# Seven products of block sums in layer 0's last product as well, and later TensorE steps for mLSTM's sums

## The chip, the cores and the metric

The kernel runs on one core of a Trainium2 chip, as one launch. The metric is the device time of that launch in microseconds (us). TensorE (PE in the profile) multiplies; VectorE (DVE), ScalarE (ACT) and GpSimd (POOL) do the elementwise work; SyncE (SP) issues nearly all DMAs, in the order in which they were put into its queue. Every engine works through its instructions in order.

## The reference

The program is a decoder trunk of two residual layers on 256 tokens of width 1024, in float32. Layer 0 mixes the tokens with an mLSTM of 4 heads, layer 1 with causal attention of 8 heads; a SwiGLU network with 2816 hidden columns stands behind each.

```python
for layer in range(2):
    u = rmsnorm(h, norm_mix[layer])
    y = mlstm_mixer(u, ...) if layer == 0 else moba_mixer(u, ...)
    h = h + y
    h = h + swiglu(rmsnorm(h, norm_ffn[layer]), ffn_w_in[layer], ffn_w_out[layer])

def swiglu(u, w_in, w_out):
    gt, up = jnp.split(u @ w_in, 2, axis=-1)
    return (jax.nn.silu(gt) * up) @ w_out
```

In the mLSTM, sums over time of the forget gates and a running maximum give the decay weights of each head; those weigh the products of queries and keys, which then multiply the values. "Layer 0's last product" is `(silu(gt) * up) @ w_out` of layer 0: 256 rows by 2816 by 1024.

## The kernel before

**Numbers.** Every factor of a large product is held as two float16 parts, a high one and a low one, and each block product is three matmuls of 512 columns: high times high, high times low, low times high. Weights come from memory as float32 pieces of 128x2048 (tile `raw`, 5 buffers). ScalarE writes a piece's high part (`wh`), VectorE its low part (`wl`), 1024 columns at a time; both have 8 buffers. `Weights.ahead` runs while the program is being written out and puts these loads and conversions between the other work. A counter `owed` says how many pieces may be loaded, each time a buffer has been read for good. `take` hands out the next converted pieces and `free` gives their buffers back.

**The order of the work.** The program is written in the order in which TensorE works. `Pace` keeps an estimated clock of TensorE (`pace.now`) and of the other engines. A `Chain` is a row of steps on several engines; each is put into its engine's queue when by these estimates its input is ready. `pace.when(test, fn)` runs `fn` as soon as the test holds at the estimated time. `follows` uses it for the mLSTM's small steps that need TensorE: `cumsum` (tile `pf`), `cummax` (`pr`), four `decay` steps (`arg`), `maxcol` (`pm`), each after the chain of the step before. They are put between the matmuls of the key and value projections (`ak`, `av`); `scores` (`qk`) and `attend_a` (`num`, `den`) come behind them.

**The feed-forward network.** `ffn(l, ...)` computes 11 groups of 256 hidden columns for both halves of the tokens (`hidden`, tile `gu`: a float32 product `fh`, its parts `n` on ScalarE and VectorE, and one transposing DMA into `hT`). Then follows the last product over 11 pieces of 256 hidden columns (tiles `f0o` and `f1o`): pieces 0 to 6 for all four blocks of the output, 2 by 2 of 128 rows by 512 columns, and then four tail pieces, first for token half 0 and then for half 1, so that the residual sum and the next norm of half 0 run beside the tail of half 1. Layer 1's projections (`b`) come right behind.

**Seven products.** A plain piece is a product of 2 by 2 blocks by 2 by 2 blocks: eight block products, 24 matmuls. In layer 1, pieces 0, 1, 3 and 5 (`SEVEN`) take seven block products of sums of blocks instead (`block`, 21 matmuls, on the four output banks and on four more, `win...`). The sums of the weights' blocks are made by VectorE from the float32 piece into a `raw` buffer of their own (`Weights.add`, four subtractions) and converted as a piece of their own (a `None` in `specs`). The sums of the hidden blocks are made in `sums_of` (tile `fs`, four steps, then the parts and a transposing DMA into `hsT`). At the end a chain named `more` adds the four extra banks onto the residual.

Of the kernel before, what the change touches and what calls it, by code (L numbers as in the profile page):

```python
# [12 lines left out]
F16 = mybir.dt.float16  # L13
# [7 lines left out]
P = 128  # L21
# [31 lines left out]
RAWBUFS, WBUFS = 5, 8  # L53


SEVEN = (0, 1, 3, 5)


START = [
# [150 lines left out]
def trunk(ctx: ExitStack, tc: tile.TileContext, a: dict, out: bass.AP):  # L210
    pace = Pace()
# [45 lines left out]
    for w, cols in ((wa, (VCOL, 0, A_SQ, VCOL + 512, OCOL, OCOL + 512)), (wb, [g * SB + i * 512 for i, g in  # L257
                    ((0, 0), (0, 1), (1, 0), (1, 1), (0, 2), (1, 2))])):
        l = 0 if w is wa else 1
        specs += [in_rows(w, c, half) for c in cols for half in range(2)]  # L260
        specs += [out_rows((a["a_w_out"], a["b_w_out"])[l][0], i) for i in range(KD // 2)]
        specs += [ffn_rows(a["ffn_w_in"][l], f, half) for f in range(NFF // 2) for half in range(2)]
        for i in range(NFF // 2):
            specs.append(out_rows(a["ffn_w_out"][l], i))
            if l == 1 and i in SEVEN:

                summed.add(len(specs))
                specs.append(None)

    class Weights:  # L270
# [24 lines left out]
        def add(self):  # L295

            i, j = self.adds.pop(0)
            (b11, b12, b21, b22), t = ([r[:, x * 512:(x + 1) * 512] for x in range(4)] for r in self.raws[i - 1:i + 1])
            x, y = ((b12, b11), (b22, t[0]), (b22, b12), (b21, t[1]))[j]
            nc.vector.tensor_tensor(t[j], x, y, op=ALU.subtract)  # L300
            self.landed[i] = pace.end

        def half(self, n):

# [11 lines left out]
        def low(self):  # L316

            i, sl = self.lows // 2, self.half(self.lows)
            h, l = self.parts[i]
            nc.vector.scalar_tensor_tensor(l[:, sl], self.raws[i][:, sl], WS, h[:, sl], op0=ALU.mult, op1=ALU.subtract)  # L320
            self.lows += 1
            self.owed += 1 - self.lows % 2

        def load_owed(self, whole=False):
            if self.owed and len(self.raws) < len(specs):
# [392 lines left out]
    part = pa.tile([A_H, S], BF16, name="part")  # L718
    mtodo, mdone = [], {}

    def follows(name, made, chain=None, test=None):


        def run():
            mdone[name] = made()

        job = pace.when(lambda: (chain is None or chain() is not None and chain().through()) and (test is None or test()), run)
        mtodo.append((name, job, chain))

    def ensure(name):  # L730
# [193 lines left out]
    for g in range(2):  # L924
        w = ws.take_k(2, 4)
        for t in range(NT):
            b = xbank(f"a{'qk'[g]}{t}")
            proj_tok(b, u, w, t)
            qk_done(g, t, b)
            if (g, t) == (0, 0):  # L930
                nc.vector.tensor_scalar(gh, gr, WS, None, op0=ALU.mult)
                nc.vector.scalar_tensor_tensor(gl, gr, WS, gh, op0=ALU.mult, op1=ALU.subtract)
            if (g, t) == (0, 1):
                prev = "gates"
                mdone["gates"] = gates()
                for name, made in [("cumsum", cumsum), ("cummax", cummax)] + [
                        (f"arg{h}", lambda h=h: decay(h)) for h in range(A_H)] + [("maxcol", maxcol)]:
                    follows(name, made, lambda prev=prev: mdone.get(prev))
                    prev = name
        ws.free(2)  # L940

# [98 lines left out]
    def ffn(l, u, j1, u_next, gain, middle):  # L1040
# [8 lines left out]
        def hidden(f, t, w):  # L1049
            b = (xbank, ybank)[t](f"gu{l}{f}{t}")  # L1050
            proj_tok(b, u, w, t, steps=3)
            sg = pfp.tile([P, 256], F32, tag="fsg", bufs=2, name=f"fsg{l}{f}{t}")
            nc.scalar.activation(sg, b[:, 0:256], AF.Silu, scale=1.0 / PS)
            seven = l == 1 and f in SEVEN
            hf = pfp.tile([P, 256], F32, tag="fhs" if seven else "fh", bufs=4, name=f"fh{l}{f}{t}")
            hfs[f, t] = hf

            h2 = []

            def prod():  # L1060
                nc.vector.scalar_tensor_tensor(hf, b[:, 256:512], HS / PS, sg, op0=ALU.mult, op1=ALU.mult)

            def high():
                h2.append(new16()[:, 0:512])
                nc.scalar.activation(h2[0][:, 0:256], hf, AF.Copy)

            def low():
                nc.vector.tensor_tensor(h2[0][:, 256:512], hf, h2[0][:, 0:256], op=ALU.subtract)
                flip16(hT[:, f, :, t * P:(t + 1) * P], h2[0])

            hjobs[f, t] = Chain(pace, [("DVE", prod), ("ACT", high), ("DVE", low)])
            if seven and t == 1:
                hjobs[f, 1].then = lambda: sums_of(f)

        def sums_of(f):

            x = pfp.tile([P, 512], F32, tag="fs", bufs=2, name=f"fs{f}")
            n16 = new16()

            def add():  # L1080
                (a11, a12), (a21, a22) = ([hfs[f, t][:, j * P:(j + 1) * P] for j in range(2)] for t in range(NT))
                s = [x[:, j * P:(j + 1) * P] for j in range(4)]
                for d, y, z, op in ((s[0], a21, a22, ALU.add), (s[1], s[0], a11, ALU.subtract),
                                    (s[2], a11, a21, ALU.subtract), (s[3], a12, s[1], ALU.subtract)):
                    nc.vector.tensor_tensor(d, y, z, op=op)

            def low():
                nc.vector.tensor_tensor(n16[:, 512:1024], x, n16[:, 0:512], op=ALU.subtract)
                flip16(hsT[:, SEVEN.index(f)], n16)

            sjobs[f] = Chain(pace, [("DVE", add), ("ACT", lambda: nc.scalar.activation(n16[:, 0:512], x, AF.Copy)),
                                    ("DVE", low)])


        hjobs, hfs, sjobs = {}, {}, {}
        if l == 1:
            hsT = pfp.tile([P, len(SEVEN), 8, P], F16, name="hsT")
        w = []
        for t in range(NT):
            if t == 1:  # L1100
# [16 lines left out]
        banks = [[xbank(f"f{l}o{t}{n}") for n in range(2)] for t in range(NT)]  # L1117
        npc, tail = NFF // 2, 4
        scale = 1.0 / (WS * HS)
        seven = SEVEN if l == 1 else ()  # L1120
        plain = [i for i in range(npc - tail) if i not in seven]
        begun, more = set(), {}

        def block(key, y, w, last):

# [8 lines left out]
        for i in range(npc - tail):  # L1134
            if i in seven:
# [6 lines left out]
                    [(h[:, j * 512:(j + 1) * 512], lo[:, j * 512:(j + 1) * 512]) for j in range(4)] for h, lo in pieces)  # L1142
                a11, a12 = ([x[:, 0:P] for x in hid(2 * i + j)] for j in range(2))
                a22 = [x[:, P:S] for x in hid(2 * i + 1)]
                s1, s2, s3, s4 = ([hsT[:, SEVEN.index(i), 4 * x + j, :] for x in range(2)] for j in range(4))
                end = i == seven[-1]
                for key, y, w in (("p1", a11, b11), ((0, 0), a12, b21), ((0, 1), s4, b22), ((1, 0), a22, t4),
                                  ("p6", s2, t2), ("p7", s3, t3), ("p5", s1, t1)):
# [37 lines left out]
        for t in range(NT):  # L1186
            last_layer = u_next is None
            ss = None if last_layer else new_ss(t)
            sums = []
            for ns in ((0, 1),) if t == 0 else ((0,),) if last_layer else ((0,), (1,)):  # L1190
                for j in range(2 * tail):
                    k = k0 + j
                    if len(w) <= j:
                        w += ws.take_k(1, 2)
                    hjobs[k // 2, t].finish()
                    acc_chunk(banks[t], *hid(k), w[j], t, False, k == NFF - 1, ns)
                for n in ns:
                    sums.append(residual_half(t, n, banks[t][n], scale, ss))
                    if last_layer:
                        sl = slice(n * 512, (n + 1) * 512)  # L1200
                        nc.sync.dma_start(orow[t * P:(t + 1) * P, sl], hres[t][:, sl])
            if last_layer and t == 1:

                more.finish()
                residual_half(1, 1, banks[1][1], scale)
                bs = [ybank(f"end{q}") for q in range(2)]
                for j in range(2 * tail):
                    (yh, yl), (wh, wl) = hid(k0 + j), w[j]
                    for q in range(2):
                        sl = slice(512 + q * 256, 768 + q * 256)  # L1210
                        for i, (lhs, rhs) in enumerate(((yh, wh), (yh, wl), (yl, wh))):
                            mm(bs[q][:, 0:256], lhs[:, P:S], rhs[:, sl], j == 0 and i == 0, j == 2 * tail - 1 and i == 2)
                for q, queue in enumerate((nc.sync, nc.scalar)):
                    sl = slice(512 + q * 256, 768 + q * 256)
                    nc.vector.scalar_tensor_tensor(hres[1][:, sl], bs[q][:, 0:256], scale, hres[1][:, sl],
                                                   op0=ALU.mult, op1=ALU.add)
                    queue.dma_start(orow[P:S, sl], hres[1][:, sl])
            if not last_layer:
                if job is not None:
                    job()  # L1220
                job = norm(f"f{l}", t, ss, grow, u_next, sums)
# [267 lines left out]
```

## Time and profile before

| What | us |
|---|---|
| Median of 3 runs | 543.25 |
| Lowest and highest of them | 542.76 to 544.75 |
| The profiled execution's own time | 543.92 |
| Its span, first to last instruction | 542.2 |
| TensorE's share of the span, busy | 99% |

The profiled execution is one execution; its span leaves out 1.7 us ahead of the first and behind the last instruction. Matmul durations overlap in the profile: a matmul of 512 columns is shown with 379 ns, and the next one starts sooner than that, so starts are compared here and not durations.

### The profile page before, as it was taken

What the parts mean: (1) busy time and instruction counts of PE and PEld (TensorE: products, weight loads), DVE (VectorE), ACT (ScalarE), POOL (GpSimd) and SP (SyncE); (2) the same over time, 40 slices, a digit from 0 to 9 for tenths busy, and PEclk for the clock granted to TensorE, in tenths of its full rate; (3) what the DMA queues carried; (4) which work ended last, traced back from release to release, by engine and by line L of the source; (5) the groups of instructions that cost most, each with busy time, mean ns of one, the idle gap of its engine ahead of it and who ended that gap; (6) DMA issues with size and microseconds to landing.
All of it is one profiled execution on the core that took longest, in us unless ns stands there. A gap on an engine that the chain in (4) does not pass through costs nothing.

```text
span 542.2 us, 7899 instructions
## 1 busy us (share of the span) xinstructions
PE 534.5 (99%) x2678; PEld 253.3 (47%) x2678; DVE 386.3 (71%) x599; ACT 317.2 (59%) x556; POOL 46.0 (8%) x105
## 2 busy tenths in 40 slices
PE   8989999999999999999999999999999999999997
PEld 4445644444444444444444455544444444444444
DVE  5979679588766655673358778988875665889932
ACT  6787584476455555463268996847655364555600
POOL 4400220010300000000013311000000000000000
PEclk9999999999999999999999999999999999999999
DMA  8999749969699879999329969699689989898502
GB/s 295 365 297 303 267 125 249 317 178 243 151 270 236 243 222 230 249 378 384 136 49 228 269 147 243 166 310 241 163 201 255 191 222 248 251 224 266 177 0 79
DMA packets 143081, 122.88 MB, mean 227 GB/s; under 512 B 68616, under 2 KB 113936, under 8 KB 143040
## 3 DMA queue, kind: packets, MB, share of 16 engines
q1 hardware_dynamic: 142144, 119.97, 80.5%
q0 software_dynamic: 736, 2.27, 1.5%
q8 instruction: 21, 0.34, 0.3%
q14 instruction: 20, 0.16, 0.1%
q10 hardware_dynamic: 160, 0.14, 0.1%
HBM read 106.08 MB, written 1.05 MB: 198 GB/s over the span
## 4 chain that ended last, share of the span: by engine, by line
PE 86%; DMA 7%; DVE 3%; issue 2%; ACT 1%; SPq 0%; POOL 0%; POOLq 0%; DVEq 0%; ACTq 0%
PE gu L228 40%; PE f0o L228 11%; PE b L228 8%; PE f1o L228 7%; PE ao L228 6%; DMA raw<-in_a_w_in 6%; PE bv L228 4%; PE av L228 2%; PE winp L228 2%; PE bo L228 1%; DVE wl L184 1%; DMA u_f<-n 1%; PE end L228 1%; PE s L228 1%; PE ak L228 1%
## 5 line engine op out<-in xcount | busy, mean ns | idle before, releaser
L184 DVE SCALAR_TENSOR_TENSOR wl<-raw,wh 128x1024 f16<-128x1024 f32 (+1 forms) x208 | 243.2, 1196 | 36.9 <-ACT wh L184 36.2
L184 ACT ACTIVATE wh<-raw 128x1024 f16<-128x1024 f32 (+1 forms) x208 | 207.8, 1029 | 82.2 <-DMA raw<-in_ffn_w_in 38.3
L228 PE MATMUL gu<-wh,u_f 128*128 128x512 f16 x704 | 209.9, 379 | 0.6 <-DMA u_f<-n 0.6
L228 PEld LDWEIGHTS <-u_f 128*128 128x128 f16 x1056 | 103.2, 98 | 125.4 <-DMA u_f<-n 1.1
L228 PE MATMUL gu<-wl,u_f 128*128 128x512 f16 x352 | 133.4, 379 | 0.0
L228 PEld LDWEIGHTS <-h 128*128 128x128 f16 x492 | 48.1, 98 | 53.1
L228 PE MATMUL f0o<-wh,h 128*128 128x512 f16 x176 | 46.6, 379 | 0.0
L184 DVE SCALAR_TENSOR_TENSOR fh<-gu,fsg 128x256 f32<-128x256 f32 x44 | 18.6, 423 | 35.0 <-ACT fsg L184 34.9
L228 PEld LDWEIGHTS <-u_a 128*128 128x128 f16 x336 | 28.7, 98 | 31.2 <-issue 0.8
L228 PEld LDWEIGHTS <-u_b 128*128 128x128 f16 x288 | 27.8, 98 | 32.0
L228 PE MATMUL b<-wh,u_b 128*128 128x512 f16 x128 | 38.9, 379 | 0.0
L184 ACT ACTIVATE n<-fh 128x256 f16<-128x256 f32 x44 | 18.2, 414 | 28.4 <-DVE fh L184 23.1
L228 PE MATMUL f1o<-wh,h 128*128 128x512 f16 x112 | 31.8, 379 | 0.0
L228 PE MATMUL f0o<-wl,h 128*128 128x512 f16 x88 | 27.4, 379 | 0.0
L184 ACT ACTIVATE fsg<-gu 128x256 f32<-128x256 f32 x44 | 16.4, 373 | 18.3 <-PE gu L228 18.2
L184 DVE TENSOR_TENSOR n<-fh,n 128x256 f16<-128x256 f32 x44 | 18.6, 423 | 10.2 <-ACT n L184 10.1
L228 PE MATMUL b<-wl,u_b 128*128 128x512 f16 x64 | 24.3, 379 | 0.0
L184 ACT ACTIVATE junk<-x 128x512 f32<-128x512 f32 x14 | 8.8, 629 | 25.2 <-DVE x L184 23.3
L184 POOL TENSOR_TENSOR r<-s,mhalf 128x1 f32<-128x1 f32 x8 | 4.5, 562 | 215.1 <-DVE s L184 215.1
L228 PE MATMUL bv<-wh,u_b 128*128 128x512 f16 x64 | 20.0, 379 | 0.0
L228 PE MATMUL ao<-wh,u_a 128*128 128x512 f16 x64 | 19.8, 379 | 0.0
L228 PE MATMUL av<-wh,u_a 128*128 128x512 f16 x64 | 19.7, 379 | 0.0
(208 smaller groups left out, 539.0 us busy)
## 6 DMA issues: line engine op xcount, KB each, us to landing
raw<-in_ffn_w_in SPq DMA_DIRECT2D x176, 256.0 KB, 4.5
raw<-in_ffn_w_out SPq DMA_DIRECT2D x88, 256.0 KB, 4.4
raw<-in_a_w_in SPq DMA_DIRECT2D x48, 256.0 KB, 5.5
raw<-in_b_w_in SPq DMA_DIRECT2D x48, 256.0 KB, 5.4
raw<-in_a_w_out SPq DMA_DIRECT2D x16, 256.0 KB, 5.7
raw<-in_b_w_out SPq DMA_DIRECT2D x16, 256.0 KB, 4.0
x<-in_x SPq DMA_DIRECT2D x4, 256.0 KB, 3.3
grow<-in_norm_ffn POOLq DMA_DIRECT2D x2, 512.0 KB, 5.4
```

The costliest lines, as they stand in the source:

```text
L184: return fn(*args, **kw)
L228: nc.tensor.matmul(dst, lhsT, rhs, start=start, stop=stop)
```

## The change

`SEVEN` becomes a pair, one tuple for each layer, and layer 0 has the same four pieces as layer 1. So `specs` gets four more pieces of weight sums in layer 0, `hidden` keeps float32 products for `sums_of` there, `hsT` exists in both layers, and the loop of the last product takes the branch with seven products. `more.finish()` moves ahead of the residual sums. `owed` is counted differently: a piece whose blocks are summed counts as read only when its four subtractions are put out too. `follows` gets a `slack`: a step is put out not when its input is ready by the estimate, but 1.5 us (`cumsum`) or 0.4 us (the other six) later.

```diff
-SEVEN = (0, 1, 3, 5)
+SEVEN = ((0,1,3,5),(0,1,3,5))
...
-            if l == 1 and i in SEVEN:
+            if i in SEVEN[l]:
                 summed.add(len(specs))
                 specs.append(None)
...
             nc.vector.tensor_tensor(t[j], x, y, op=ALU.subtract)
             self.landed[i] = pace.end
+            if j == 3 and self.lows >= 2 * i:
+                self.owed += 1
+
+        def summing(self, i):
+            return i + 1 in summed and (i + 1 >= len(self.raws) or any(q[0] == i + 1 for q in self.adds))
...
             self.lows += 1
-            self.owed += 1 - self.lows % 2
+            if self.lows % 2 == 0 and not self.summing(i):
+                self.owed += 1
...
-    def follows(name, made, chain=None, test=None):
+    def follows(name, made, chain, slack):
...
-        job = pace.when(lambda: (chain is None or chain() is not None and chain().through()) and (test is None or test()), run)
+        job = pace.when(lambda: chain() is not None and chain().through() and pace.now >= chain().ready + slack, run)
...
-                    follows(name, made, lambda prev=prev: mdone.get(prev))
+                    follows(name, made, lambda prev=prev: mdone.get(prev), 1.5 if name == "cumsum" else 0.4)
...
-            seven = l == 1 and f in SEVEN
+            seven = f in SEVEN[l]
...
-        if l == 1:
-            hsT = pfp.tile([P, len(SEVEN), 8, P], F16, name="hsT")
+        if SEVEN[l]:
+            hsT = pfp.tile([P, len(SEVEN[l]), 8, P], F16, name="hsT")
...
-        seven = SEVEN if l == 1 else ()
+        seven = SEVEN[l]
...
                     acc_chunk(banks[t], *hid(k), w[j], t, False, k == NFF - 1, ns)
+                if more:
+                    more.finish()
                 for n in ns:
                     sums.append(residual_half(t, n, banks[t][n], scale, ss))
...
             if last_layer and t == 1:
-                more.finish()
                 residual_half(1, 1, banks[1][1], scale)
```

## Rows read from the trace of the kernel before

**Rows 1.** The page: the span, the busy time of the engines (share of the span, instructions), TensorE's granted clock in 40 equal slices (9 is 90% or more of full speed), and the shares of the chain that ended last.
```profile
span 542.2 us, 7899 instructions
PE 534.5 (99%) x2678; PEld 253.3 (47%) x2678; DVE 386.3 (71%) x599; ACT 317.2 (59%) x556; POOL 46.0 (8%) x105
...
PEclk9999999999999999999999999999999999999999
...
PE 86%; DMA 7%; DVE 3%; issue 2%; ACT 1%; SPq 0%; POOL 0%; POOLq 0%; DVEq 0%; ACTq 0%
```

**Rows 2.** The chain that ended last, in order of time: start, us, what. First layer 0's hidden products and its last product, then the start of layer 1's last product.
```profile
106.30 113.96 PE gu L228 x528
220.26 56.98 PE f0o L228 x264
...
484.16 0.65 PE winp L228 x3
```

**Rows 3.** Busy time of each engine (instructions in brackets) in four stretches: pieces 0 to 6 of layer 0's last product, from its first matmul to the first of the tail; its tail, to the first matmul of `b`; pieces 0 to 6 of layer 1's last product, from its first matmul to the first of the tail; layer 0's hidden products. Columns: stretch, length, then PE, PEld, DVE, ACT, POOL, TensorE's granted clock, DMA share, GB/s.
```profile
220.10:256.36 36.26, 36.26 (x170) 16.45 (x169) 21.32 (x19) 18.21 (x19) 0.00 (x0) 1.00 0.96 338
256.36:277.08 20.72, 20.72 (x98) 9.38 (x97) 7.23 (x10) 6.38 (x11) 0.57 (x1) 1.00 0.45 137
484.00:517.67 33.67, 33.67 (x157) 15.25 (x156) 33.16 (x40) 19.36 (x23) 0.00 (x0) 1.00 0.64 208
100.00:220.00 120.00, 119.83 (x558) 54.40 (x557) 81.04 (x116) 67.79 (x102) 8.42 (x34) 1.00 0.88 229
```

**Rows 4.** Groups of instructions by shape, with busy us, mean ns and idle time before them: TensorE's weight loads (PEld) in pieces 0 to 6 of layer 0 (the first row) and of layer 1 (the other two).
```profile
L228 PEld LDWEIGHTS <-h 128*128 128x128 f16 x167 | 16.4, 98 | 19.7
...
L228 PEld LDWEIGHTS <-h 128*128 128x128 f16 x107 | 10.5, 98 | 12.6
L228 PEld LDWEIGHTS <-hsT 128*128 128x128 f16 x48 | 4.7, 98 | 5.7
```

**Rows 5.** Groups by shape over the whole run: what the four pieces with seven products cost VectorE and ScalarE in layer 1 (two kinds of the weights' low parts, of 1024 and of 512 columns; one of the two groups of the weights' sums; one of the four groups of the hidden sums; their two parts; one group of the four extra banks' way onto the residual), and the issues of the transposing DMA with the median us to landing.
```profile
L184 DVE SCALAR_TENSOR_TENSOR wl<-raw,wh 128x1024 f16<-128x1024 f32 x196 | 234.3, 1221 | 36.9 <-ACT wh L184 36.2 <-issue 0.3
L184 DVE SCALAR_TENSOR_TENSOR wl<-raw,wh 128x512 f16<-128x512 f32 x12 | 9.1, 789 | 0.0
L184 DVE TENSOR_TENSOR raw<-raw,raw 128x512 f32<-128x512 f32 x8 | 5.5, 686 | 0.3 <-DMA raw<-in_ffn_w_out 0.2
L184 DVE TENSOR_TENSOR fs<-fs,fh 128x128 f32<-128x128 f32 x4 | 1.2, 292 | 0.1
L184 DVE TENSOR_TENSOR n<-fs,n 128x512 f16<-128x512 f32 x4 | 2.8, 690 | 0.9 <-ACT n L184 0.8
L184 ACT ACTIVATE n<-fs 128x512 f16<-128x512 f32 x4 | 2.5, 628 | 2.4 <-DVE fs L184 2.0 <-ACT fsg L184 0.4
L184 DVE SCALAR_TENSOR_TENSOR x<-winp,x 128x512 f32<-128x512 f32 x3 | 2.1, 690 | 0.1
...
hsT<-n SPq DMA_TRANSPOSE x4, 4.4
```

**Rows 6.** TensorE's instructions in order of time around `cumsum` (start, us, what, and in brackets the idle time before and what ended it): the last matmul of `ak` ahead of it, its first matmul, the next matmul of `ak`, and `cummax`.
```profile
38.27 0.38 PE L228 MATMUL ak<-wh,u_a 128*128 128x512 f16 x1
40.13 0.35 PE L228 MATMUL pf<-lf,triu 128*128 128x4 f32 x2 [1.48 <-DVE lf L184]
...
40.79 0.38 PE L228 MATMUL ak<-wh,u_a 128*128 128x512 f16 x1
...
42.08 0.38 PE L786 MATMUL pr<-ident,acol 128*4 128x128 f32 x2
```

**Rows 7.** VectorE's instructions in order of time: a weight conversion in the middle of the gates' steps, the step that gives `lf` to `cumsum`, a run of four conversions, and the first weighing of the scores.
```profile
37.90 1.22 DVE L184 SCALAR_TENSOR_TENSOR wl<-raw,wh 128x1024 f16<-128x1024 f32 x1
...
39.81 0.17 DVE L184 SCALAR_TENSOR_TENSOR lf<-gate,sp 128x8 f32<-128x8 f32 x1
...
47.33 4.62 DVE L184 SCALAR_TENSOR_TENSOR wl<-raw,wh 128x1024 f16<-128x1024 f32 x4
52.56 0.56 DVE L184 SCALAR_TENSOR_TENSOR pt<-qk,wt 128x384 f32<-128x384 f32 x1 [0.60 <-PE qk L228]
```

**Rows 8.** What the first scores wait for: the issue of the keys' last transposing DMA, its time from issue to landing, the first scores on TensorE, VectorE's last step of head 0's weights, and the first matmul of `attend_a`.
```profile
47.45 1.24 SPq L551 DMA_TRANSPOSE kT<-n  x1
...
DMA to landing us min/median/max: 3.5/3.5/3.5
...
51.87 0.66 PE L228 MATMUL qk<-qT,kT 128*128 128x256 f16 x6
...
54.15 0.55 DVE L184 TENSOR_TENSOR p<-pt,p 128x384 f16<-128x384 f32 x1
...
55.11 0.27 PE L228 MATMUL num<-vah,p 128*128 128x256 f16 x1
```

**Rows 9.** The end of layer 0's last product: VectorE's last two conversions of layer 1's weights, the residual sums of token half 0, the issue of the two transposing DMAs of its norm, the first one's time to landing, and the first matmul of layer 1 that reads it.
```profile
257.64 2.36 DVE L184 SCALAR_TENSOR_TENSOR wl<-raw,wh 128x1024 f16<-128x1024 f32 x2 [2.82 <-ACT wh L184]
266.70 1.29 DVE L184 SCALAR_TENSOR_TENSOR x<-f0o,x 128x512 f32<-128x512 f32 x2 [6.70 <-PE f0o L228]
...
272.04 2.84 SPq L551 DMA_TRANSPOSE u_b<-n  x2
...
DMA to landing us min/median/max: 3.0/3.0/3.0
...
277.08 0.38 PE L228 MATMUL b<-wh,u_b 128*128 128x512 f16 x1
```

More of the change, by code (lines that the diff above doesn't have):

```diff
@@ L1088, in low @@
                 nc.vector.tensor_tensor(n16[:, 512:1024], x, n16[:, 0:512], op=ALU.subtract)
-                flip16(hsT[:, SEVEN.index(f)], n16)
+                flip16(hsT[:, SEVEN[l].index(f)], n16)
             sjobs[f] = Chain(pace, [("DVE", add), ("ACT", lambda: nc.scalar.activation(n16[:, 0:512], x, AF.Copy)),
@@ L1119, in ffn @@
         scale = 1.0 / (WS * HS)
-        seven = SEVEN if l == 1 else ()
+        seven = SEVEN[l]
         plain = [i for i in range(npc - tail) if i not in seven]
-        begun, more = set(), {}
+        begun, more = set(), None
         def block(key, y, w, last):
@@ L1144, in ffn @@
                 a22 = [x[:, P:S] for x in hid(2 * i + 1)]
-                s1, s2, s3, s4 = ([hsT[:, SEVEN.index(i), 4 * x + j, :] for x in range(2)] for j in range(4))
+                s1, s2, s3, s4 = ([hsT[:, seven.index(i), 4 * x + j, :] for x in range(2)] for j in range(4))
                 end = i == seven[-1]
```

## The prediction

> **What bounds the kernel now.** I read the page first. TensorE is busy for 534.5 of 542.2 us at the full granted clock in every slice, and 86% of the chain that ended last is TensorE's; VectorE is busy for 71% [rows 1]. A busy TensorE in this profile need not be a TensorE at its peak, since its matmuls overlap, so I next read the chain in order of time. Layer 0's last product stands there as one piece, 264 matmuls in 56.98 us, which is 215.8 ns from start to start, and the 528 hidden matmuls ahead of it take 215.8 ns each too [rows 2]. So TensorE runs there without a hole, and what the end moves by is what TensorE saves or newly waits for. Third, the timeline of TensorE in the first 60 us, where the steps of mLSTM's sums lie; last, the ends of the stretches that a faster TensorE might run into.
>
> **Part 1: seven products in layer 0.** Each of the four pieces has 21 matmuls for 24, so 12 go: 12 x 215.8 ns = 2.59 us. Layer 1 shows the same thing already done. Its pieces 0 to 6 take 33.67 us from the first matmul to the first of the tail, layer 0's take 36.26 us, and the difference is 2.59 us, although VectorE is busy for 33.16 of the 33.67 us there [rows 3]. So this term holds as long as TensorE is not kept waiting.
>
> A plain piece loads one set of stationary columns for two matmuls, a piece of seven products one for each matmul: in all 36 more weight loads of 98 ns [rows 4]. In layer 1 they lie beside matmuls, since 4 x 21 + 3 x 24 = 156 matmuls at 215.8 ns are the whole 33.67 us [rows 3, 4]. I cost them at nothing; without that cover they would be 36 x 98 ns = 3.5 us. The Trainium skill ("TensorE: Matmul & The Clock Gate", "Part 3: Packing small matmuls — row/col tiling") says that a weight load overlaps a running matmul only when it goes to another group of rows of the array. Every load here fills the whole array, so by that rule the change would pay these 3.5 us; the trace disagrees, as the 33.67 us show.
>
> VectorE's new work, by rows of layer 1 [rows 5]. Weights: four subtractions of 0.686 us for each of four pieces, 11.0 us. Low parts: a plain piece has two of 1.22 us, one of seven products has three and one of about 0.7 to 0.8 us, so about 2.0 us more for each, 8 us. The way of the four banks to the residual: nine steps of 0.69 us, 6.2 us. Together 25 us around the last product. Hidden sums: four steps of 0.29 and one of 0.69 us for each piece, 7.4 us, beside layer 0's hidden products. In those VectorE is busy for 81 of 120 us, and in the last product and its tail it is idle for 14.9 + 13.5 = 28.4 us [rows 3]. The new work fits into the idle time, closely in the second stretch; a part of it is done earlier, since weights are converted ahead of their use. ScalarE gets 0.63 us for each of the hidden sums [rows 5] and some more high parts, in stretches where it is busy for about half [rows 3]. SP's queue gets four more transposing DMAs, 4.4 us to landing [rows 5]; the weight loads behind them are pushed back by little more than an issue of 1.24 us, as one of this kind lasts in [rows 8]. I cost all this at nothing, hidden behind TensorE's 113.96 and 56.98 us [rows 2]. If VectorE is late, TensorE waits for a low part; layer 1, with VectorE full, shows no such wait.
>
> The counter `owed` moves some loads of both layers behind the four subtractions. A load then no longer stands in SP's queue waiting for a buffer that VectorE still reads, ahead of transposing DMAs that could go. No TensorE time hangs on it while weights are ahead, so nothing. `more.finish()` only forces what is left of that chain into VectorE's queue ahead of the first residual sum; between piece 5's end and that sum TensorE has 24 + 48 matmuls, 15.5 us, against 6.2 us of steps. Nothing.
>
> **Part 2: the steps of mLSTM's sums.** TensorE's last matmul ahead of `cumsum` starts at 38.27, so the next could start at 38.48; `cumsum` starts at 40.13, since VectorE gives `lf` at 39.98 [rows 6, 7]. That is 1.65 us lost, and no other instruction of TensorE between 38 and 43 us shows idle time ahead of it [rows 6]. VectorE is late because conversions stand between the gates' steps: one of 1.22 us at 37.90, in the middle of them [rows 7]. With 1.5 us of slack some seven matmuls of `ak` go in front, 7 x 0.216 = 1.51 us, and `cumsum` itself still runs near 40.1. So at most 1.5 us of the 1.65 come back here.
>
> What is late next: VectorE, ScalarE and the DMAs do not run earlier than before, while TensorE arrives everywhere 1.5 us earlier. The first scores start at 51.87. They need the keys' last transposing DMA, issued at 47.45 and landed 3.5 us later, at 50.95 [rows 8]; there is 0.92 us of room. VectorE works through conversions until 51.95 and starts on the scores at 52.56 [rows 7], 0.6 us of room, and its last step for head 0 ends at 54.70, 0.41 us ahead of the first matmul of `attend_a` [rows 8]. These two in a row are 1.0 us of room. So of the 1.5 us about 0.5 us would be lost again at the scores or at `attend_a`, and about 1.0 us stays. The 0.4 us of slack on the other six steps moves each behind some two more matmuls; `cummax`, the first of them, showed no idle time before [rows 6], so I put them at nothing. The bounds: 0, if the later waits take everything back, and 1.65 us, the whole hole. I take 1.0 us, as the rooms in [rows 7, 8] lie nearer to the upper end. No loss, as a wait that only takes back what TensorE gained ahead of it cannot make more than that.
>
> **Sum.** 543.92 us of the profiled execution less 2.59 less 1.0 is 540.3. That execution lies 0.67 us above the median of 543.25, so against the median 539.7 us, 0.65% faster.
>
> **Rivals.**
> *The second part comes to nothing.* TensorE meets the keys' DMA, the scores' weights and whatever else VectorE owes until about 60 us, and only the first part stays: 543.25 - 2.6 = 540.65, with a rest of up to 0.4 us of gain about 540.3 to 541.0. For it: VectorE has no idle time from 47.33 to 51.95 [rows 7]. Against it: the rooms worked out above.
>
> *Layer 1's start becomes late (the other side).* Layer 1's first matmul, at 277.08, reads what the first DMA of half 0's norm lands: 272.04 + 3.0 = 275.04, some 2 us of room [rows 9]; from the residual sum at 266.70 on, that chain hardly waits. Before, VectorE is idle for 6.70 us ahead of it, since the last two conversions of layer 1's weights end at 260.00 [rows 9]. The change fills that gap with most of its 25 us. The tail holds four of the eight buffers for converted pieces, so four pieces of layer 1, eight conversions, fit in before its end. If VectorE then still owes all eight, 8 x 1.22 = 9.8 us [rows 5] stand ahead of the residual sum, and TensorE waits 9.8 - 2.0 = 7.8 us: 539.7 + 7.8 = 547.5. It decides from 2 us of backlog on, and ends above the time before from 5.6 us on. Against it: layer 1 gets through the like work of its own last product in 33 us [rows 3], and layer 0 enters its last product with more weights ready. A weak form of it, one or two conversions too many, gives 540 to 542.
>
> *Weight loads that show.* If the 36 more loads stood between the matmuls, the time would be 539.7 + 3.5 = 543.2: no change. Layer 1's 33.67 us for 156 matmuls speak against it [rows 3]. It is what the rule of the Trainium skill told above would give.
>
> *The first part isn't delivered.* The converted pieces or the hidden sums of layer 0 come late and TensorE waits for as much as it saves: 543.25 - 1.0 = 542.25. Against it: in layer 1 the same four pieces come in time, and VectorE has 39 us idle in layer 0's hidden products [rows 3].
>
> **How the numbers follow.** Both parts, with 0.5 to 1.65 us from the second, 539.0 to 540.2: 0.65, and the likeliest value is 539.7. The second part gone: 0.18. Layer 1's start late: 0.10, of which 0.05 in the strong form. Weight loads 0.02, first part not delivered 0.05. Half a per cent of 543.25 is 2.7 us, which is about what a measurement can tell from no change, so faster means below 540.5. The first case lies there; of the second about a quarter does. Faster 0.67, same 0.28, slower 0.05. The range goes from 538.6, where the whole hole of 1.65 us comes back (543.25 - 2.59 - 1.65 = 539.0) and the runs scatter a little, to 542.3, which takes in the second case, the weak form of the third and the last.
>
> **What would show it.** Layer 0's pieces 0 to 6 should take 33.7 us for 36.26, with no hole in TensorE, and VectorE should be nearly full there. `cumsum` should start within 0.3 us of the end of the matmul before it, with some seven more matmuls of `ak` ahead of it. If I am wrong about the rest, a new wait for the keys' DMA or for head 0's weights of more than 1 us will stand between 50 and 56 us. Layer 1's first matmul should follow the tail within 0.3 us; a hole there with VectorE busy ahead of the residual sum is the third case. If the first part fails, holes lie between matmuls of layer 0's last product, ended by low parts or by `hsT`.

## The result and the profile after

The changed kernel takes 540.55 us (median of 6 runs, 539.42 to 541.36), the kernel before 543.16 us beside it. The ratio is 0.9949 with a 95% interval of 0.9932 to 0.9966, 2.6 us or 0.5% faster. 539.7 us had been forecast. In its own stretch of the trace the first part of the sum arrived to a hundredth of a microsecond (2.58 us for 2.59); the second did not arrive at all.

The page of the kernel after: its span, the engines' busy time and the chain's shares, as in [rows 1]:

```profile
span 539.7 us, 7963 instructions
PE 532.0 (99%) x2666; PEld 252.0 (47%) x2666; DVE 412.7 (76%) x652; ACT 324.8 (60%) x568; POOL 46.5 (9%) x105
...
PEclk9999999999999999999999999999999999999999
...
PE 88%; DMA 9%; SPq 1%; issue 1%; ACT 1%; DVE 0%; DVEq 0%; ACTq 0%
```

TensorE has twelve instructions fewer and 2.5 us less of busy time; VectorE has 53 more and 26.4 us more, against 25 + 7.4 us in the forecast. This profiled execution took 541.36 us, 0.8 us above its median; that of before lay 0.67 us above 543.25 us.

Busy time in three of the stretches of [rows 3], here of after: layer 0's pieces 0 to 6, its tail, layer 1's pieces 0 to 6.

```profile
220.98:254.66 33.68, 33.68 (x158) 15.25 (x156) 33.17 (x40) 23.98 (x28) 0.00 (x0) 1.00 0.95 317
254.66:275.38 20.72, 20.72 (x98) 9.41 (x96) 16.00 (x18) 8.22 (x13) 0.57 (x1) 1.00 0.77 258
481.87:515.56 33.69, 33.69 (x158) 15.28 (x156) 33.18 (x40) 19.34 (x23) 0.00 (x0) 1.00 0.63 206
```

Layer 0's row has become that of layer 1: 33.68 us for 36.26, TensorE busy throughout, VectorE busy for 33.17 us. Here all that was wanted has been delivered. In the tail VectorE is busy for 16.0 of 20.7 us (7.2 before).

The second part shows on TensorE's timeline around `cumsum` and `cummax`, and at the first scores (start, us, what; in brackets the idle time before and what ended it):

```profile
39.68 0.38 PE L228 MATMUL ak<-wh,u_a 128*128 128x512 f16 x1
40.34 0.36 PE L228 MATMUL pf<-lf,triu 128*128 128x4 f32 x2 [0.28 <-DVE lf L184]
...
42.73 0.38 PE L228 MATMUL ak<-wh,u_a 128*128 128x512 f16 x1
43.40 0.38 PE L793 MATMUL pr<-ident,acol 128*4 128x128 f32 x2 [0.29 <-DVE acol L184]
...
50.66 0.49 PE L228 MATMUL qk<-qT,kT 128*128 128x256 f16 x3
51.76 0.34 PE L228 MATMUL qk<-qT,kT 128*128 128x128 f16 x3 [0.60 <-DMA kT<-n]
```

The brackets count from the modelled end of the matmul before; what TensorE loses is the distance from start to start above the 0.216 us (smaller for small matmuls) that it has without a wait. That is 0.45 us at `cumsum` (40.34 - 39.68 - 0.216), 0.45 us at `cummax`, 0.77 us inside the first scores: 1.67 us. Before, it was the one hole of 1.65 us in [rows 6]. The hole has been split in three. That the two sums are so nearly equal is chance: further down, other executions of either order show other sizes.

VectorE in the same microseconds:

```profile
40.03 0.17 DVE L184 SCALAR_TENSOR_TENSOR lf<-gate,sp 128x8 f32<-128x8 f32 x1
40.11 1.22 DVE L184 SCALAR_TENSOR_TENSOR wl<-raw,wh 128x1024 f16<-128x1024 f32 x1
...
41.85 1.21 DVE L184 SCALAR_TENSOR_TENSOR wl<-raw,wh 128x1024 f16<-128x1024 f32 x1
42.99 0.16 DVE L184 COPY fcum<-pf 128x8 f32<-128x8 f32 x1
43.18 0.17 DVE L184 TENSOR_TENSOR acol<-gate,fcum 128x8 f32<-128x8 f32 x1
...
47.30 0.69 DVE L184 SCALAR_TENSOR_TENSOR n<-ak,n 128x512 f16<-128x512 f32 x1 [0.36 <-ACT n L184]
```

`lf` ends at 40.20, where before it ended at 39.98 [rows 7]. `pf` is finished by about 41.1, but `fcum` and `acol`, which `cummax` needs, stand behind the conversion of 41.85 and end at 43.35. And ScalarE, at the high part of the last piece of the keys, whose last matmul started at 44.69:

```profile
45.73 1.06 ACT L184 ACTIVATE wh<-raw 128x1024 f16<-128x1024 f32 x1 [1.53 <-DMA raw<-in_a_w_in]
46.69 0.58 ACT L184 ACTIVATE n<-ak 128x512 f16<-128x512 f32 x1
```

The high part stands in ScalarE's queue behind a conversion that waits for a load until 45.73. So the low part comes at 47.30, and the keys' last transposing DMA, as the answer for `kT` shows it, later than at 47.45 with 3.5 us to landing [rows 8]:

```profile
L558 SPq DMA_TRANSPOSE kT<-n x1: 1232/1232/1232, 48.0 to 48.0; - x1
...
DMA to landing us min/median/max: 3.7/3.7/3.7
```

Before, the high part stood behind such a conversion as well, but its load had landed 0.6 us earlier:

```profile
45.12 1.06 ACT L184 ACTIVATE wh<-raw 128x1024 f16<-128x1024 f32 x1 [1.21 <-DMA raw<-in_a_w_in]
46.08 0.58 ACT L184 ACTIVATE n<-ak 128x512 f16<-128x512 f32 x1
```

ScalarE is not the whole of it: VectorE, which writes the low part, is busy with the steps of `cummax` until 46.94, so it waits for ScalarE only the last 0.36 us.

Last, the end of layer 0's last product, VectorE first and then TensorE, as in [rows 9]:

```profile
257.92 5.76 DVE L184 SCALAR_TENSOR_TENSOR wl<-raw,wh 128x1024 f16<-128x1024 f32 x5
265.00 1.29 DVE L184 SCALAR_TENSOR_TENSOR x<-f0o,x 128x512 f32<-128x512 f32 x2 [1.33 <-PE f0o L228]
...
275.16 0.38 PE L228 MATMUL f0o<-wh,h 128*128 128x512 f16 x1
275.38 0.38 PE L228 MATMUL b<-wh,u_b 128*128 128x512 f16 x1
```

VectorE's idle time ahead of the residual sum has shrunk from 6.70 to 1.33 us, and layer 1's first matmul follows without a hole. The rival on the other side didn't happen, but the room is almost gone. The first DMA of the norm, which that matmul reads, in the kernel after:

```profile
L558 SPq DMA_TRANSPOSE u_b<-n x1: 1247/1247/1247, 271.8 to 271.8; - x1
...
DMA to landing us min/median/max: 3.2/3.2/3.2
```

It landed at 275.0 us, 0.4 us ahead of the matmul at 275.38; before, 2.0 us were left there [rows 9].

One hole had not been thought of. At the second token half of layer 0's hidden products TensorE waits for the norm's transposed DMAs (the chain, in order of time: start, us, what):

```profile
110.81 6.52 DMA u_f<-n
117.33 0.05 issue
117.38 103.77 PE gu L228 x480
221.15 0.65 PE winp L228 x3
```

That costs 1.08 us. Before, two of these three DMAs landed in 4.1 and 4.9 us without a hole there, but 0.75 us were lost at the same point of layer 1. At layer 0's `u_f`, the three traces without the later steps (before, and two of the kernels below) have no hole; of the nine with them seven have one, of 0.19 to 1.08 us. So by these traces this place, too, takes back some of what the later steps gain. At layer 1's, holes come and go in either.

### The profile page after: what moved, and what is told of

Its sections match the earlier page's. It is cut to its first block, busy times and chain, and to the rows that moved or that the text cites. A ratio compares the mean times of both kernels' runs of the same rounds, so it can differ in the third digit from the quotient of the medians.

```text
span 539.7 us, 7963 instructions
## 1 busy us (share of the span) xinstructions
PE 532.0 (99%) x2666; PEld 252.0 (47%) x2666; DVE 412.7 (76%) x652; ACT 324.8 (60%) x568; POOL 46.5 (9%) x105
## 4 chain that ended last, share of the span: by engine, by line
PE 88%; DMA 9%; SPq 1%; issue 1%; ACT 1%; DVE 0%; DVEq 0%; ACTq 0%
PE gu L228 40%; PE f0o L228 8%; PE ao L228 8%; PE b L228 8%; PE f1o L228 7%; DMA raw<-in_a_w_in 7%; PE bo L228 4%; PE winp L228 4%; PE bv L228 4%; DMA u_f<-n 1%; PE av L228 1%; PE end L228 1%; PE s L228 1%; PE num L228 1%; PE o L228 1%
## 5 line engine op out<-in xcount | busy, mean ns | idle before, releaser
L184 DVE SCALAR_TENSOR_TENSOR wl<-raw,wh 128x1024 f16<-128x1024 f32 (+1 forms) x216 | 248.2, 1183 | 18.7 <-ACT wh L184 18.3
L184 ACT ACTIVATE wh<-raw 128x1024 f16<-128x1024 f32 (+1 forms) x216 | 213.3, 1021 | 62.1 <-DMA raw<-in_ffn_w_in 32.8
L228 PEld LDWEIGHTS <-h 128*128 128x128 f16 x432 | 42.3, 98 | 46.1
L228 PE MATMUL f0o<-wh,h 128*128 128x512 f16 x128 | 36.6, 379 | 0.0
L228 PE MATMUL f0o<-wl,h 128*128 128x512 f16 x64 | 21.0, 379 | 0.0
```

The source lines that it names most:

```text
L184: return fn(*args, **kw)
L228: nc.tensor.matmul(dst, lhsT, rhs, start=start, stop=stop)
```

## The experiments

**Each part alone, and neither.** Three kernels, with the changed kernel and the one before as the two corners. One keeps the seven products and sets the slack to 0:

```
-  follows(name, made, lambda prev=prev: mdone.get(prev), 1.5 if name == "cumsum" else 0.4)
+  follows(name, made, lambda prev=prev: mdone.get(prev), 0.0)
```

> The seven products in layer 0 and the new counter, with the steps of mLSTM's sums put out as in the kernel before (no slack). Theory A (the change is worth 12 matmuls and nothing else; the later steps only move a hole): 2.5 to 2.7 us under the kernel before, as the changed kernel is, with one hole of about 1.65 us ahead of cumsum and none at the first scores. Theory B (the later steps are worth about 1 us, and the first part delivers only about 1.6): 1.4 to 1.8 us under the kernel before.

The second keeps the slacks and takes layer 0's four pieces out:

```
-SEVEN = ((0,1,3,5),(0,1,3,5))
+SEVEN = ((),(0,1,3,5))
```

> The later steps alone (and the new counter); layer 0 has no piece of seven products. Theory A: the same as the kernel before within 0.5 us, with holes of about 0.4, 0.4 and 0.8 us ahead of cumsum, of cummax and inside the first scores, 1.6 us in all, in place of one of 1.65. Theory B: 1.0 us or more under the kernel before.

The third does both edits, so that only the changed bookkeeping of `owed` and the earlier place of `more.finish()` are left.

> Neither part: only the new counter of loads and the earlier place of the chain of the four extra banks, both in layer 1. If loads put out behind the four subtractions cost or give nothing, the same as the kernel before within 0.3 us. If they matter, a difference of 0.5 us or more, and holes in layer 1's last product or fewer of them.

Measured, beside 542.87 us of before: the seven products alone 540.34 us, ratio 0.9949 (0.9935 to 0.9962), which is the whole change. The later steps alone 543.36 us, 1.0006 (0.9997 to 1.0015). Neither 542.88 us, 1.0001 (0.9992 to 1.0009). So the second part is worth nothing with the first or without it. Of the bookkeeping the third kernel says nothing: its trace has the same instructions in the same order on every engine as that of before, so without layer 0's pieces the new counting moves nothing. It is the kernel before run once more, and shows how much one execution differs from the next. TensorE in the kernel with the later steps alone:

```profile
40.16 0.28 PE L228 MATMUL pf<-lf,triu 128*128 128x4 f32 x2
...
42.81 0.38 PE L793 MATMUL pr<-ident,acol 128*4 128x128 f32 x2
...
50.07 0.49 PE L228 MATMUL qk<-qT,kT 128*128 128x256 f16 x3
51.16 0.34 PE L228 MATMUL qk<-qT,kT 128*128 128x128 f16 x3 [0.60 <-DMA kT<-n]
```

Here the slack does what it says: no wait at `cumsum`, almost none (0.13 us) at `cummax`. TensorE then comes to the scores at 50.07, and loses 0.76 us in them; 1.08 us more go at 116.79, for `u_f`. With neither edit, `cumsum` waits 0.81 us by the bracket, 0.97 us from start to start, and the scores, at 51.39, wait for nothing:

```profile
39.65 0.35 PE L228 MATMUL pf<-lf,triu 128*128 128x4 f32 x2 [0.81 <-DVE lf L184]
...
51.39 0.66 PE L228 MATMUL qk<-qT,kT 128*128 128x256 f16 x6
```

That is the trade without the first part: 0.97 us saved at `cumsum`, 0.13 + 0.76 us paid at `cummax` and the scores. One execution gives the places, but not the sizes. In the old order `cumsum` alone waited 1.65 us (before), 1.68 us (the seven products alone) and 0.97 us (neither). The order with the later steps is the same up to 57 us in five of the kernels here, and the three places together cost 1.67 us (the change), 0.89 us (the later steps alone), and 1.55, 0.39 and 0.81 us (with five pieces, with six, and with the waiting clock, all below). What moves the hole at `cumsum` stands further up the chain that ended last: a weight load, here before and with neither edit:

```profile
28.71 5.33 DMA raw<-in_a_w_in
...
28.23 5.35 DMA raw<-in_a_w_in
```

They landed at 34.04 and 33.58 us, and `lf` ended 5.9 us behind that in both, at 39.98 and 39.51 us. So VectorE's conversions are not the only reason why `lf` is late.

**The scores later, too.** If the scores are merely emitted too early, moving them back by 0.9 us lets `av` fill the wait:

```
-  return all(c.through() for c in qchains.values()) and ...
+  return all(c.through() and pace.now >= c.ready + 0.9 for c in qchains.values()) and ...
```

> The changed kernel, with the scores of each head put out 0.9 us later on the estimated clock, some five matmuls of the value projection further back. Theory A says that the hole of 0.77 us inside the first scores is the wait for the keys' last transposing DMA: it goes, and the time is 0.5 to 0.8 us under that of the changed kernel, 3.1 to 3.4 us under the kernel before. Rival: it comes back one step on, at head 0's weights ahead of attend_a, and the time stays within 0.3 us of the changed kernel's.

539.96 us, ratio 0.9941 (0.9929 to 0.9954): its interval overlaps that of the change, and the wait did not go. The second half of the scores starts at 51.96, 1.15 us late, behind the keys' DMA issued at 48.28. The clock by which the order is laid out had the keys landed; on the chip ScalarE took their high part at 46.95. A later place by an estimate does not help where the estimate misses the wait for a load.

**No conversions ahead of the keys.** This takes the cause away: from `cumsum` on nothing is converted ahead until the keys' low part has been emitted.

```
+        ws.hold = True                 # in cumsum()
+        if (g, t) == (1, 1):           # where the chain of q and k is made
+            qchains[g, t].then = lambda: setattr(ws, "hold", False)
             ...
+            if self.hold:              # in ahead(), behind the loads
+                return
```

> The changed kernel, with no conversion of weights put into VectorE's and ScalarE's queues from cumsum on until the keys' last low part is put out (loads go on). Theory A says that the keys' last transposing DMA is late because the keys' high part stands on ScalarE behind a conversion that waits for a load, and VectorE's steps of the sums behind conversions. Then the DMA is issued 1 us or more earlier after the end of ak than in the changed kernel (there 3.0 us after it), the holes at cummax and inside the first scores (0.45 and 0.77 us) go, and the time is about 1.0 us under the changed kernel's, 3.4 to 3.8 us under the kernel before. Rival: the DMA itself is late, or the conversions put off are missed later: the hole stays or another one appears, and the time is within 0.3 us of the changed kernel's.

540.53 us, ratio 0.9957 (0.9944 to 0.9971). The first half worked: ScalarE takes the high part at 44.52, and the DMA is issued at 46.5, 1.5 us earlier than after. The second did not:

```profile
L560 SPq DMA_TRANSPOSE kT<-n x1: 1232/1232/1232, 46.5 to 46.5; - x1
...
DMA to landing us min/median/max: 4.5/4.5/4.5
```

It took 4.5 us to land for 3.7, and VectorE's low part waited until 45.80 behind the steps of `cummax`. TensorE came earlier by 0.6 us and lost 0.70 us in the scores, 0.34 us at `cummax` and 0.75 us at `u_f`. So conversions in front of the keys delay the issue of that DMA, but taking them away wins no time: over these kernels the DMA took between 3.1 and 4.5 us to land, a difference as large as the gain looked for.

**One piece more.** The first part turned VectorE's spare time into TensorE time at a known rate, so how much is left? Five pieces of layer 0, then six, and five with the hold above and more slack at `cumsum` (the diff is of `SEVEN`, here of the first; in the third also `2.1 if name == "cumsum"` and the lines of the hold):

```
-SEVEN = ((0,1,3,5),(0,1,3,5))
+SEVEN = ((0,1,3,5,6),(0,1,3,5))
```

> The changed kernel with piece 6 of layer 0's last product as a fifth piece of seven products. If TensorE alone sets the time there, three matmuls less: 0.65 us under the changed kernel, about 3.25 us under the kernel before, no hole in pieces 0 to 6 or at layer 1's start. If VectorE is at its end already (it has 5.2 us of work more in the last product, and 1.3 us of idle time ahead of the residual sum in the changed kernel), a hole of 1 us or more ahead of layer 1's first matmul or in the tail.

> The changed kernel with pieces 4 and 6 of layer 0's last product as fifth and sixth pieces of seven products. TensorE saves six matmuls more, 1.3 us. VectorE gets some 10 us more of work there, where the changed kernel's weights are ready 6.7 us ahead of their use at the least. Theory: VectorE becomes the bound, the weights' lead is used up from piece 5 on, holes of 1 to 4 us appear, and the time is the same as or above that of the kernel with five pieces. Rival: the idle time of VectorE in the tail takes it up, and the time is 1.3 us under the changed kernel.

> Put together: no conversions from cumsum to the keys' low part, cumsum put out 2.1 us later for 1.5, and five pieces of seven products in layer 0. If the gains add up: 1.0 us from the first, 0.3 to 0.4 us from the rest of the hole ahead of cumsum, 0.65 us from the fifth piece, so 1.9 to 2.1 us under the changed kernel, 4.5 to 4.7 us under the kernel before, with no hole of more than 0.3 us between 30 and 60 us.

Beside 542.84 us of before: five pieces 559.87 us, ratio 1.0310 (1.029 to 1.0329); six pieces 659.02 us, 1.2135 (1.209 to 1.2179); five with the hold 602.63 us, 1.1101 (1.1078 to 1.1125). Where four pieces win 2.6 us, the fifth loses 19. The expectation for five had a hole ahead of layer 1's first matmul, and that came (1.08 us); it had nothing of the other 18 us. For five with the hold, 1.9 to 2.1 us below the changed kernel had been expected; there TensorE waits more than 0.5 us for a weight from 350 us on, against 436 us without the hold, and why so much earlier was not followed. In the kernel with five pieces, layer 0's last product itself has no hole. Layer 1 has them, and far from the change, in its hidden products and its last product:

```profile
436.22 0.38 PE L228 MATMUL gu<-wh,u_f 128*128 128x512 f16 x1 [0.99 <-ACT wh L184]
437.48 0.38 PE L228 MATMUL gu<-wl,u_f 128*128 128x512 f16 x1 [0.88 <-DVE wl L184]
...
503.58 0.38 PE L228 MATMUL f1o<-wh,h 128*128 128x512 f16 x1 [1.65 <-ACT wh L184]
504.84 0.38 PE L228 MATMUL f1o<-wl,h 128*128 128x512 f16 x1 [0.88 <-DVE wl L184]
```

A weight's high part comes late, the low part right behind it, then the next weight. Two causes are possible. Either layer 1's engines cannot carry the work, or its order cannot recover: the order is laid out by a clock that counts TensorE's work alone, and `take` forces a late conversion into the queues without that clock going on. By the count taken while the order is laid out, the changed kernel has 1.5 to 3 blocks of weights converted ahead of use from block 75 to block 104; with five pieces it is 0 from block 80 to the end, and from 76 to 90 `owed` stands at 3 or 4, buffers that are free and not loaded. No load was lost from `owed`: at the end it stands at 5, the number of buffers, in the changed kernel and in those with five and six pieces.

**The clock that waits.** To tell these apart, `take` lets the clock go on to the end of a conversion that it had to force (from weight block 36 on); five pieces as before. A second kernel also has six raw buffers for five and seven pairs of converted ones for eight.

```
                 self.low()
+                if self.taken >= 36 and pace.end > pace.now:
+                    pace.spend(pace.end - pace.now)
```

> Five pieces of layer 0 summed, as in the run with (0,1,3,5,6) that took 559.87 us, and one line more: where a block of weights is not ready when TensorE's matmuls are emitted, the clock by which the instructions are ordered goes on to the end of that conversion (from weight block 36 on), so that loads and conversions go on being emitted in the wait. Theory one (the fifth piece takes the lead of the conversions, and the emitted order then never gives it back, because its clock knows of no wait): the lead comes back in layer 1's early products, holes there sum to 2 to 5 us, none behind 420 us, and the time is 540.5 - 0.65 + 2 to 5 = 542 to 545 us. Theory two (VectorE, ScalarE or the transfers cannot carry the fifth piece's work in layer 1): the holes stay through layer 1, and the time is 555 to 560 us.

> The same with six buffers for the raw weights (five before) and seven for the converted ones (eight before). Theory one: transfers can run one block further ahead, the estimated lead in layer 1's last product is 2 blocks against 0.5 to 1.5, so the time is that of the run before it or up to 2 us less, 540 to 545 us. Theory two: as before, 555 us and more. A third view, that the buffers for the converted weights are what the lead needs, gives a longer time than the run before it, 545 to 550 us.

544.18 us, ratio 1.0029 (1.0017 to 1.0041), and 545.15 us, 1.0042 (1.0028 to 1.0056), beside 542.99 us. One line of bookkeeping wins back 15.7 of the 19 us, in the range of the first theory; the engines can carry five pieces, the order could not. For the second kernel the first theory had the same time or up to 2 us less, and that missed: 0.97 us more, at the foot of the third view's range, though the two intervals overlap and do not decide it. Most of what is left of five pieces' loss stands at two places in the kernel with the waiting clock, and neither wait is ended by a weight's part:

```profile
274.71 0.39 PE L228 MATMUL b<-wh,u_b 128*128 128x512 f16 x1 [0.94 <-DMA u_b<-n]
310.55 0.49 PE L228 MATMUL s<-bkT,bqT 128*128 128x256 f16 x3 [1.77 <-DMA bkT<-n]
```

1.10 and 1.94 us, from start to start. The second is not in the kernel with five pieces and without the waiting clock; where it comes from was not followed. The first is the rival of the late start of layer 1. VectorE ahead of it, in the same kernel:

```profile
264.26 0.69 DVE L184 SCALAR_TENSOR_TENSOR x<-winp,x 128x512 f32<-128x512 f32 x1
264.86 1.28 DVE L184 SCALAR_TENSOR_TENSOR x<-f0o,x 128x512 f32<-128x512 f32 x2
...
268.63 0.69 DVE L184 SCALAR_TENSOR_TENSOR x<-f0o,x 128x512 f32<-128x512 f32 x1 [1.24 <-PE f0o L228]
269.24 1.40 DVE L184 SCALAR_TENSOR_TENSOR u_f<-x,r,grow 128x512 f32<-128x512 f32 x2
```

There is no idle time ahead of the residual sum (1.33 us with four pieces, 6.70 without). It starts at 264.86, as late as with four (265.00), while TensorE is ready for `b` 1.77 us earlier. The fifth piece saves TensorE 0.65 us and takes more than the last idle time that VectorE had ahead of that sum. But behind it VectorE still stands idle for 1.24 us: the norm's step `u_f` is queued behind a residual sum of half 1 that waits for TensorE (before, that sum stood behind the norm's steps, at 272.55). That wait alone is longer than the hole of 1.10 us, so the hole may come from the order and not from a VectorE that is full; no run tried the other order, nor the waiting clock with four pieces. Of the versions that ran, four pieces are best, and none beats the changed kernel by more than the intervals.

## Why the prediction was right and where not

**Part 1, 2.59 us: right, by its own working.** 36.26 became 33.68 us, and the seven products alone give the whole gain. The weight loads cost nothing: 156 full ones and as many matmuls take 33.68 us, 215.9 ns each, in layer 0 as in layer 1. One sentence of the Trainium skill ("TensorE: Matmul & The Clock Gate", "Part 3: Packing small matmuls — row/col tiling"), that a weight load overlaps running matmuls only where it goes to another group of rows, would make 3.5 us more due; the trace disagrees a second time. The same section of the Trainium skill also lets a load into a background weight buffer go ahead of running matmuls, which the prediction left out and with which the trace agrees. VectorE's cost, 32 us by the rows of layer 1, measured 26.4 us over the run, and it fitted in; the sum added up single durations, and these overlap in the profile (four conversions of 1.22 us take 4.62 us [rows 7]).

**`owed` and `more.finish()` at nothing: not contradicted, and not tested apart.** The kernel with neither edit has the order of before, so its ratio of 1.0001 says nothing of them. With layer 0's pieces in, 2.5 of the 2.59 us arrive in the median, so what they cost is not seen within the interval.

**Part 2, 1.0 us: wrong, it measured nothing (1.0006, 0.9997 to 1.0015, by itself).** The bound of 0 was named, and the rival "the second part comes to nothing" gave 540.65 us for 540.55 measured, with a chance of 0.18. The stated range held because it took that rival in, and not because the sum was right. The step that failed is the one that worked out 0.92 and 0.6 us of room at the scores. Several things went wrong in it. It took the keys' DMA to be issued and landed as before, 47.45 + 3.5 = 50.95; it landed at 51.7 after and, in the other kernels, as much as 4.5 us from its issue; the scores waited for it in every trace with the later steps and in none without them. ScalarE's wait for a load in front of the high part of the keys, 1.21 us in the trace of before already, was not looked up at all. It put `cummax` at nothing because it showed no idle time before; with `cumsum` no longer late, `acol` became late, 0.45 us. And it took the hole of 1.65 us for a fixed size, some seven matmuls; six moved, and `lf` itself came 0.22 us later, so 0.45 us of the old hole were left (none in the kernel with the later steps alone, in the same order). Room was measured against one execution's clock times of other queues, and those times move with the loads from one execution to the next, and again when the order is laid out anew.

**"No loss" of part 2: as forecast,** within 1.0006 (0.9997 to 1.0015).

**Layer 1 late: not at four pieces, as forecast; the point from which it decides was told too far out.** 2 us of room had been worked out, on the ground that the chain behind the residual sum hardly waits. VectorE's idle time of 6.70 us fell to 1.33, but that chain grew too, by 1.4 us up to the issue of its DMA: a residual sum of half 1, which waits for TensorE, came ahead of the norm's low part on VectorE. The room fell to 0.4 us. With a fifth piece the hole came, 1.1 us. What the forecast did not have is the larger loss behind it: an order that never gives a lost lead back, 15.7 us.

**The signs named:** 33.7 us in layer 0, yes. `cumsum` within 0.3 us of the matmul ahead, yes by the bracket (0.28), with six matmuls more, not seven. A wait of over 1 us between 50 and 56 us as the sign of a wrong second part: no, 0.77 us, although the second part was wrong; the rest went at the two small ones ahead of it and at `u_f`. `b` within 0.3 us: yes.

What stays open is what sets the landing time of the keys' and the norm's transposing DMAs. The traces show it longer in some kernels and do not tell what each one stood behind. Also open is how the later steps' gain is divided, in the mean of many executions, among the places that take it back: each kernel left one trace.

## What to carry to other kernels

Where the bounding engine's stream has no hole, instructions taken out of it are worth their start-to-start distance, and a stage that already has the change gives the price to a hundredth; check only that the engine that pays has idle time ahead of the next chain, how much of it is left, and what else stands in that chain. A hole at one of several waits in a row is worth what is left at the last of them: take its size from more than one execution, follow each queue behind it, with its waits for loads, and expect nothing from moving the first alone. Where the order is laid out by an estimated clock, a wait that the clock doesn't know of can turn a small shortage into a lasting one.

## What the runs showed of the hardware that was not expected

In some executions TensorE ran at the lower of its two clocks (1.2 for 2.4 GHz) for a few microseconds in the middle of the run, behind holes of one to two microseconds in the two kernels told here. In the kernel with the seven products alone, behind the hole of 1.68 us at `cumsum`, its timeline and the granted clock of that stretch (the column behind POOL's) are:

```profile
40.59 0.36 PE L228 MATMUL pf<-lf,triu 128*128 128x4 f32 x2 [1.52 <-DVE lf L184]
...
42.81 0.63 PE L228 MATMUL ak<-wh,u_a 128*128 128x512 f16 x1
43.24 0.63 PE L793 MATMUL pr<-ident,acol 128*4 128x128 f32 x2
43.66 0.63 PE L228 MATMUL ak<-wh,u_a 128*128 128x512 f16 x1
```

```profile
41.70:45.30 3.60, 3.60 (x11) 1.36 (x10) 3.12 (x7) 2.46 (x3) 0.00 (x0) 0.53 1.26 310
```

Eight matmuls there have 427 ns from start to start for 216, so that 1.7 us are lost on top of the hole. With five pieces the same happened twice, from 457.7 to 460.9 and from 505.1 to 508.7 us, each behind a pair of holes of 1.0 to 1.8 us. So a hole can cost more than its length, but need not: that of the kernel before, 1.65 us, and that of 1.94 us in the kernel with the waiting clock were not followed by such a stretch.

A transposing DMA of one size took 3.1 to 6.5 us to land within one execution, that of after: 3.1 and 3.2 us for `u_b` at 272 us, 3.7 us for `kT` at 48 us, 6.0 and 6.5 us for two of the three of `u_f` around 111 us.
